# Walking the columns of two feed-forward parts in runs taken from both halves of the tile

## The chip, the cores and the metric

The kernel runs on one core of one Trainium2 chip. The metric is the device time of one execution in microseconds, and lower is better. Engines are named as the profile names them: PE is TensorE (PEld its weight loads), DVE is VectorE, ACT is ScalarE, POOL is GpSimd, SP issues the DMAs.

## The reference

Two layers of a diffusion transformer in float32 on two streams of 256 tokens, the latent `x` and the context `ctx`, each 1024 wide. Each layer is a feed-forward part, a token mixer (a gated recurrence, an mLSTM and a windowed attention, merged by gates) and a second feed-forward part. Every part has a norm in front, which shift and scale by the conditioning, and a gate behind. Cut to what matters:

```python
def swiglu(h, w1, w3, w2):
    return (jax.nn.silu(h @ w1) * (h @ w3)) @ w2

xl, xc = x, ctx
for l in range(DEPTH):                      # DEPTH = 2
    ctx_out = l < DEPTH - 1
    ml, mc = ...                            # modulations from c and c_ctx
    xl = xl + 0.5 * ml[:, :, 2] * swiglu(ln_mod(xl, ...), ffn_w1[l, 0], ffn_w3[l, 0], ffn_w2[l, 0])
    xc = xc + 0.5 * mc[2] * swiglu(ln_mod(xc, ...), ffn_w1[l, 0], ffn_w3[l, 0], ffn_w2[l, 0])
    yl, yc = token_mixer(ln_mod(xl, ...), ln_mod(xc, ...), ..., ctx_out)
    xl = xl + ml[:, :, 5] * yl
    xl = xl + 0.5 * ml[:, :, 8] * swiglu(ln_mod(xl, ...), ffn_w1[l, 1], ffn_w3[l, 1], ffn_w2[l, 1])
    if ctx_out:
        xc = xc + mc[5] * yc
        xc = xc + 0.5 * mc[8] * swiglu(ln_mod(xc, ...), ffn_w1[l, 1], ffn_w3[l, 1], ffn_w2[l, 1])
return xl
```

The inner width of a feed-forward part is 2816, which is 22 chunks of 128.

## The kernel before

Features lie on the 128 partitions and tokens along the columns. A tile of activations is 512 columns wide: columns 0 to 255 are the latent stream (`LAT`), 256 to 511 the context stream (`CTX`), and `BOTH` is all of them. A PSUM bank holds one such tile in float32.

Products keep float32 accuracy with operands of type float32r: each operand is split into a high and a low part, and one chunk of 128 of the contraction is three matmuls, high by high, high by low and low by high (`mm3`, L255 to L263). The weights are the stationary operand, a 128x128 block for each matmul. The activations are the moving operand, `hh` and `hl` (the normed input) or `gh` and `gl` (the inner activations), and the three matmuls add into `ps`. In the profile a matmul of the first kind stands under L261, of the second under L262, of the third under L263.

A feed-forward part (`ffn`, L565) goes through the inner width in three thirds of 8, 7 and 7 chunks (`THIRDS`, L24). In each third, the up products of a chunk make two banks, `p1` and `p3` (L600, L601; the profile writes `p`), over 8 chunks of the contraction; ACT and DVE turn them into `gh` and `gl`. The down products (`dn`, L623 and L638) then contract over the third's 8 or 7 chunks into 8 chunks of the residual. With both streams, up and down products take all 512 columns in one matmul, with two exceptions: the first three chunks of the first third are taken stream by stream (256 columns) where the norm ends stream by stream (`proj_first`, L517, with `BY_STREAM`), and so are the last five chunks of the residual in the last third (`passes_of`, L536).

Of the four feed-forward parts, `(l, j)` = (0, 0), (0, 1) and (1, 0) have both streams; (1, 1) has the latent stream alone, with 256 columns. Parts (0, 1) and (1, 0) follow each other directly, and the mixer of layer 1 follows part (1, 0). In that mixer, `unit` (L1151) makes most products over 256 columns, but nine over 512: three of the keys `k`, four of the values `v`, one each of the attention's keys and values (L1172 to L1179), each of 8 chunks and so 24 matmuls.

PE's order is the program's own (`manual_schedule`, L92). The small products of the norms and of the mixer's chains stand between the large ones at places that a step count sets (`tick`, L158), from fixed durations for a product and not from measured ones. Weights come by DMA on SP's queue into three buffers and are split by ACT (L246) and DVE (L247), some products ahead of their use. DVE also works off the conditioning (L387) beside the first three feed-forward parts.

Of the kernel before, what the change touches and what calls it, by code (L numbers as in the profile page):

```python
# [17 lines left out]
T = 512  # L18
# [15 lines left out]
PREP = 3  # L34
LATER = 300
# [4 lines left out]
# steps of the side chains per microsecond of large products, by layer  # L40
# [8 lines left out]
# columns of the constant array  # L49
# [10 lines left out]
# columns of the per-layer vectors  # L60
V_G = 0            # 3 x 8 x 2
V_ADAB = 48        # 72 x 2
V_CW = 192         # 4 chunks x 4 taps
V_CB = 208
V_BA = 212         # d x c
# [6 lines left out]
V_SINK = 243       # 8  # L72
# [4 lines left out]
# projection chunks of w_in in the order in which they are used  # L77
# [6 lines left out]
def body(ctx, tc, ins, out):  # L84
# [29 lines left out]
    def give(n):  # L114
        """n more slots for weights (or fewer, n < 0)"""
        for _ in range(n):
            free[0].append(free[1].pop(0))
        for _ in range(-n):
            free[1].append(free[0].pop())

# [1 line left out]
    banks = [list(range(PE_MAIN)), list(range(PE_MAIN, 8))]  # L122
# [13 lines left out]
    def pgive(n):  # L136
        """n more banks for the large products (or fewer, n < 0)"""
        a, b = (1, 0) if n > 0 else (0, 1)
        for _ in range(abs(n)):
            banks[b].append(banks[a].pop(0))  # L140

    # ---- small work that runs beside the large products. The tensor engine works in the order of this program:
    # what needs it waits for the end of a large product, so that its operands are there when its turn comes ----
# [4 lines left out]
    def defer(n, f):  # L148
        """call f after n large products"""
        later.append([n, f])  # L150

    def start(gen, rate):
        """a chain of steps; rate: steps per microsecond of large products"""
        ch = [gen, rate, 0.0]
        chains.append(ch)
        return ch
# [83 lines left out]
    def split_w(r, n):  # L240
        """[128, n] weights, chunks of 128 rows side by side -> float32r parts in tiles of 4 chunks"""
        w = []
        for a in range(0, n, 512):
            e = min(n - a, 512)
            hi, lo = salloc("whi", F32R, 0), salloc("wlo", F32R, 0)
            S.copy(hi[:, :e], r[:, a:a + e])  # L246
            V.tensor_tensor(lo[:, :e], r[:, a:a + e], hi[:, :e].bitcast(F32), op=ALU.subtract)  # L247
            w.append((hi, lo))
        return w
# [4 lines left out]

    def mm3(ps, w, kk, xh, xl, cols, ks=None, koff=0):  # L255
        """ps[:, cols] (+)= w.T x in float32 accuracy: high x high + high x low + low x high"""
        for k in (range(kk) if ks is None else ks):
            hi, lo = w[(k + koff) // 4]
            ws = slice((k + koff) % 4 * P, (k + koff) % 4 * P + P)
            o = ps[:, cols]  # L260
            PE.matmul(o, hi[:, ws], xh[k][:, cols], start=(k == 0), stop=False)  # L261
            PE.matmul(o, hi[:, ws], xl[k][:, cols], start=False, stop=False)  # L262
            PE.matmul(o, lo[:, ws], xh[k][:, cols], start=False, stop=(k == kk - 1))  # L263

    def mm3_beside(ps, w, kk, xh, xl, cols):
        """the same, with a place for small work in the middle; the caller ticks the second half"""
        h = kk // 2
        mm3(ps, w, kk, xh, xl, cols, range(h))
        tick(pe_us(cols, h))
        mm3(ps, w, kk, xh, xl, cols, range(h, kk))  # L270

    def split_act(src, cols=BOTH, name="y"):
        """float32 data in two float32r slots"""
        hi = salloc(name + "h", F32R)
        lo = salloc(name + "l", F32R)
        split_into(hi, lo, src, cols)
        return hi, lo
# [6 lines left out]
    def ada_load(h):  # L284
        """a quarter of the weights of the first two modulations, by chunk of the contraction"""
        src = ins["ada0"]
        if h % 2:
            ts = [salloc("ada0") for _ in range(KD)]
            for k in range(KD):
                nc.sync.dma_start(ts[k][:, :T], src[h, :, k * T:(k + 1) * T])  # L290
            return [(t, 0) for t in ts], lambda: sfree(*ts)
        ts = [ada_tile(src[h, :, i * D:(i + 1) * D]) for i in range(2)]
        r = raw_tile(src[h, :, 2 * D:4 * D], 2 * D)
        return [(ts[k // 2], k % 2 * T) if k < 4 else (r, (k - 4) * T) for k in range(KD)], lambda: None

    def ada_first(w, ps, ks):
        """their products on the idle tensor engine, four column groups at once"""
        for k in ks:
            t, o = w[0][k]
            for j in range(4):  # L300
                PE.matmul(ps[32 * j:32 * j + 32, 0:P], cT[:, k, :], t[:, o + j * P:o + (j + 1) * P],
                          start=(k == 0), stop=(k == KD - 1))
# [19 lines left out]
    def ada_second():  # L322
        """the next modulation on the tensor engine, in steps"""
# [29 lines left out]
    def cond_load():  # L353
        """silu of both conditioning vectors, on every partition"""
# [14 lines left out]
    def ada_steps():  # L369
        """the modulations: features on partitions, sums along the rows of the turned weights"""  # L370
# [8 lines left out]
        for i, (l, m) in enumerate(ADA_MODS):  # L379
            # nothing reads the last of the second layer's for the second stream  # L380
# [31 lines left out]
    def rsqrt(v, shape):  # L412
        """v ** -0.5 of a small tile: a first guess from the exponent bits, then Newton steps"""
# [41 lines left out]
    def norm_rstd(s, use, lag=2):  # L455
        """use(rows of 1 / rms on all partitions), some large products later"""
# [42 lines left out]
    # the first chunks of a projection from h, in the order in which h comes: the columns, the chunks of the  # L499
    # contraction, and how many chunks of features take turns  # L500
# [35 lines left out]
    def passes_of(streams, load, use, ahead=None, begin=None):  # L536
        """the products that end a part: the last chunks stream by stream, so that the next norm of one runs beside
        the other. load(pair of chunks), use(stream or None, chunk, weights)"""
# [26 lines left out]
    def ffn(l, j, streams, order, after, first, ahead, prep=None):  # L565
        """after(s, k): called when chunk k of the residual of stream s is complete"""
# [6 lines left out]
        for ti, (a, b) in enumerate(THIRDS):  # L573
            kk = b - a
            gh, gl = [], []
# [57 lines left out]
            def down_first(ws):  # L633
                # the newest chunk of the contraction comes last
# [32 lines left out]
    def log1p_series(o, e, tmp_alloc):  # L667
        """log(1 + e) for 0 <= e <= 1: 2 atanh(e / (2 + e))"""
# [33 lines left out]
    def rg_scan(l, xps, hs):  # L702
        """convolution, gates and hidden states of both directions, summed, chunk by chunk"""
# [19 lines left out]
        for c in range(4):  # L723
# [3 lines left out]
            for d in range(2):  # L727
# [12 lines left out]
                # log a = -2 y; q = tanh y, e = exp(-2 y) = 2 / (1 + q) - 1:  # L740
                # a = 1 - q (1 + e), sqrt(1 - a a) = sqrt(q) (1 + e)
# [37 lines left out]
    def ml_rows(l, f, li, res):  # L779
        """gate rows; per token: columns G (for keys) and exp(-m) (for queries), and -M as rows in two parts"""  # L780
# [4 lines left out]
        # log sigmoid of the forget gates, tokens on partitions  # L785
# [55 lines left out]
    def mlstm(l, q, k, v1, to, f, li, y, lat_only):  # L841
        """q, k feature-major; v1 token-major with a column of ones; to: the output gates"""
# [5 lines left out]
        for h in range(4):  # L848
# [8 lines left out]
            for s in (2, 3, 0, 1):  # L857
# [4 lines left out]
                for d in range(2):  # L862
                    # ranges of queries that see the key chunk s; the mask covers its own chunk
# [30 lines left out]
            for t in tcs:  # L894
                ps = palloc("av")
                for d in range(2):
                    # key chunks that the query chunk t sees
# [49 lines left out]
    def attention(l, k2, queries, vts, rq, y, lat_only):  # L947
# [3 lines left out]
        def scores(c, hf, g, ti):  # L951
            """softmax of one chunk of queries over its keys"""
# [27 lines left out]
        def turn(p, pt, nk, ti):  # L980
            """keys to partitions: key chunk s -> columns (s % 2, query chunk) of tile s // 2"""
# [247 lines left out]
    def attend(l, raws, sqs, vts, y, lat_only, held):  # L1229
        """Per head, the rotated queries in two float32r parts, one above the other; per key head, the normalised  # L1230
        and rotated keys, each part twice: two products over 128 rows make all of the float32 scores. The scales of
        the queries stay apart, as columns."""
# [90 lines left out]
    # ================= program =================  # L1323
# [49 lines left out]
    def prep(h):  # L1373
        """the next quarter of the first modulations and of the normed input"""
# [19 lines left out]
    def normer(l, n):  # L1394
        """squares of the new residual; at its end the norm n of layer l"""
# [37 lines left out]
def _chunk_cols(w):  # L1433
    """[K, N] -> [N / 128, 128 (k in chunk), K / 128 * 128]"""
    K, N = w.shape
    return np.ascontiguousarray(w.reshape(K // P, P, N // P, P).transpose(2, 1, 0, 3)).reshape(N // P, P, K)


def _constants():
    c = np.zeros((P, NCONST), np.float32)  # L1440
    c[:, C_ID:C_ID + P] = np.eye(P)
    # rotation: out[i] = sum_j R[j, i] x[j]
# [119 lines left out]
```

## Time and profile before

| | us |
|---|---|
| runs, median (lowest, highest) | 2230.1 (2229.87, 2230.32) |
| span of the profiled execution | 2228.2 |
| PE busy in the span | 2186.7 (98%) |
| DVE busy | 1495.2 (67%) |
| ACT busy | 1021.4 (46%) |
| mean granted TensorE clock | 0.997 |

The span goes from the first to the last instruction of the profiled execution; the median of the runs is 1.9 us above it. Times along the span are in us from its start. A matmul's busy time in the profile is longer than its share of the engine, since matmuls are pipelined: the next one starts before the one before has ended. What a matmul costs is therefore read from the distance between starts, or from a count in a stretch.

### The profile page before, as it was taken

To read this page: it belongs to the slowest core of one execution; us is meant where nothing else is said; L and a number is where in the kernel's file an instruction comes from. 1 tells how busy PE (TensorE), PEld (TensorE's weight loads), DVE (VectorE), ACT (ScalarE), POOL (GpSimd) and SP (SyncE) were. 2 spreads that over 40 slices of the span, in tenths; PEclk is the share of its full clock that TensorE was granted. 3 is DMA by queue.
4 is the path that set the end of the run, shared out by engine and by line. 5 is a ranking of instruction groups with operands and counts; after the bars stand their busy time and mean duration, and the time that the engine had idled before them with its cause. 6 is when DMAs were issued, how large, how long until landed. Compare 5 with 4: busy or idle time off the path is not lost.

```text
span 2228.2 us, 32885 instructions
## 1 busy us (share of the span) xinstructions
PE 2186.7 (98%) x12357; PEld 1856.5 (83%) x12357; DVE 1495.2 (67%) x3605; ACT 1021.4 (46%) x2021; POOL 4.7 (0%) x40
## 2 busy tenths in 40 slices
PE   6999999999999999999999999999999999998999
PEld 5778888977877778998888898888889778998999
DVE  5899834679766645689973368754346987776664
ACT  4322223468575534542222353232335887655553
POOL 0000000000000000000000000000000000000000
PEclk9999999999999999999999999999999999999999
DMA  9665522311111322445552226642222222454552
GB/s 357 227 236 209 188 92 102 109 62 64 65 57 67 114 86 95 152 160 211 210 175 103 77 89 238 247 165 95 88 93 87 88 83 97 141 181 178 209 189 86
DMA packets 74944, 310.30 MB, mean 139 GB/s; under 512 B 7072, under 2 KB 10656, under 8 KB 60704
## 3 DMA queue, kind: packets, MB, share of 16 engines
q1 hardware_dynamic: 74784, 308.19, 39.0%
q8 instruction: 97, 1.59, 0.3%
q14 instruction: 63, 0.52, 0.1%
HBM read 303.97 MB, written 4.19 MB: 138 GB/s over the span
## 4 chain that ended last, share of the span: by engine, by line
PE 91%; DVE 4%; ACT 3%; DMA 1%; issue 1%; SPq 0%; ACTq 0%; DVEq 0%
PE p L261 11%; PE p L262 11%; PE p L263 11%; PE dn L261 6%; PE dn L262 6%; PE dn L263 6%; PE pg L262 3%; PE pg L261 3%; PE pg L263 3%; PE pj L261 3%; PE pj L262 3%; PE pj L263 3%; PE up L261 2%; PE up L262 2%; PE up L263 2%; PE ao L998 1%
## 5 line engine op out<-in xcount | busy, mean ns | idle before, releaser
L246 ACT CAST whi<-raw 128x512 fp32r<-128x512 f32 (+1 forms) x844 | 506.7, 612 | 830.9 <-PE p L262 385.4
L247 DVE TENSOR_TENSOR wlo<-raw,whi 128x512 fp32r<-128x512 f32 (+1 forms) x844 | 564.2, 678 | 362.0 <-ACT whi L246 352.5
L261 PE MATMUL p<-hh,whi 128*128 128x512 f32 (+1 forms) x1216 | 445.4, 366 | 0.5 <-ACT silu L579 0.5
L262 PE MATMUL p<-hl,whi 128*128 128x512 f32 (+1 forms) x1216 | 445.6, 366 | 0.0
L263 PE MATMUL p<-hh,wlo 128*128 128x512 f32 (+1 forms) x1216 | 444.0, 365 | 0.0
L387 DVE SCALAR_TENSOR_TENSOR junk<-ada,cb 128x512 f32<-128x512 f32 x416 | 290.0, 697 | 34.8 <-DMA ada<-ada 27.7
L261 PE MATMUL dn<-gh,whi 128*128 128x512 f32 (+1 forms) x809 | 275.6, 341 | 0.0
L263 PE MATMUL dn<-gh,wlo 128*128 128x512 f32 (+1 forms) x809 | 275.1, 340 | 0.0
L262 PE MATMUL dn<-gl,whi 128*128 128x512 f32 (+1 forms) x809 | 274.9, 340 | 0.0
L261 PEld LDWEIGHTS p<-hh,whi 128*128 128x128 f32 x1216 | 228.4, 188 | 43.1 <-issue 1.2
L263 PEld LDWEIGHTS p<-hh,wlo 128*128 128x128 f32 x1216 | 228.5, 188 | 40.4
L262 PEld LDWEIGHTS p<-hl,whi 128*128 128x128 f32 x1216 | 228.5, 188 | 39.6
L262 PEld LDWEIGHTS dn<-gl,whi 128*128 128x128 f32 x809 | 152.2, 188 | 18.8
L261 PEld LDWEIGHTS dn<-gh,whi 128*128 128x128 f32 x809 | 152.2, 188 | 18.7
L263 PEld LDWEIGHTS dn<-gh,wlo 128*128 128x128 f32 x809 | 152.1, 188 | 18.7
L261 PE MATMUL pj<-hh,whi 128*128 128x512 f32 (+1 forms) x400 | 153.8, 384 | 1.2 <-DVE li L776 1.2
L262 PE MATMUL pj<-hl,whi 128*128 128x512 f32 (+1 forms) x400 | 143.9, 360 | 0.0
L263 PE MATMUL pj<-hh,wlo 128*128 128x512 f32 (+1 forms) x400 | 143.5, 359 | 0.0
L262 PE MATMUL pg<-hl,whi 128*128 128x512 f32 (+1 forms) x384 | 129.9, 338 | 0.0
L261 PE MATMUL pg<-hh,whi 128*128 128x512 f32 (+1 forms) x384 | 129.8, 338 | 0.0
L263 PE MATMUL pg<-hh,wlo 128*128 128x512 f32 (+1 forms) x384 | 129.3, 337 | 0.0
L496 DVE SCALAR_TENSOR_TENSOR x<-dn,Ga,x 128x256 f32<-128x256 f32 x168 | 74.8, 479 | 54.1 <-PE dn L263 53.4
(281 smaller groups left out, 3444.5 us busy)
## 6 DMA issues: line engine op xcount, KB each, us to landing
raw<-w SPq DMA_DIRECT2D x104, 1024.0 KB, 4.8
ada<-ada SPq DMA_DIRECT2D x124, 512.0 KB, 3.8
raw<-win SPq DMA_DIRECT2D x30, 1024.0 KB, 4.8
raw<-w SPq DMA_DIRECT2D x32, 896.0 KB, 4.6
raw<-wbr SPq DMA_DIRECT2D x24, 1024.0 KB, 4.8
raw<-wbo SPq DMA_DIRECT2D x24, 512.0 KB, 3.3
raw<-wout SPq DMA_DIRECT2D x8, 1024.0 KB, 4.7
raw<-ada SPq DMA_DIRECT2D x6, 1024.0 KB, 6.4
```

The source lines that it names most:

```text
L246: S.copy(hi[:, :e], r[:, a:a + e])
L247: V.tensor_tensor(lo[:, :e], r[:, a:a + e], hi[:, :e].bitcast(F32), op=ALU.subtract)
L261: PE.matmul(o, hi[:, ws], xh[k][:, cols], start=(k == 0), stop=False)
L262: PE.matmul(o, hi[:, ws], xl[k][:, cols], start=False, stop=False)
L263: PE.matmul(o, lo[:, ws], xh[k][:, cols], start=False, stop=(k == kk - 1))
L387: V.scalar_tensor_tensor(junk[0], r[:, e * T:(e + 1) * T], 1.0, cb[2 * s + e][:, :T], op0=ALU.mult, op1=ALU.mult, accum_out=am[:, b, s, e: ...
L496: V.scalar_tensor_tensor(x[k][:, c], ps[:, c], Gate[l, n][:, k, s:s + 1], x[k][:, c], op0=ALU.mult, op1=ALU.add)
L998: PE.matmul(po[c][rows, cc], vts[0][:, sv * P + 64 * hf:sv * P + 64 * hf + 64], pt[s // 2][:, (s % 2) * 256:(s % 2) * 256 + 256], start=(s ...
```

## The change

In `ffn`, each third sets `walk[0]` from the table `WALKS`; parts that aren't in the table set 0. In `mm3`, a product over 512 columns whose `walk[0]` is not 0 no longer goes through columns 0 to 511 in order. Its moving operand and its output are seen as `(h b r) -> b h r`: `r` columns of the first half, the same `r` columns of the second half, the next `r` of the first half, and so on. Operand and output go through the columns in the same order, so each column's result lands where it did. Products over 256 columns are as before. Comments and docstrings were dropped as well, which moves line numbers: L261 to L263 become L270 to L272.

```diff
+WALKS = {(0, 1): (128, 32, 4), (1, 0): (64, 16, 8)}
...
+    walk = [0]
+
     def mm3(ps, w, kk, xh, xl, cols, ks=None, koff=0):
         for k in (range(kk) if ks is None else ks):
             hi, lo = w[(k + koff) // 4]
             ws = slice((k + koff) % 4 * P, (k + koff) % 4 * P + P)
-            o = ps[:, cols]
-            PE.matmul(o, hi[:, ws], xh[k][:, cols], start=(k == 0), stop=False)
-            PE.matmul(o, hi[:, ws], xl[k][:, cols], start=False, stop=False)
-            PE.matmul(o, lo[:, ws], xh[k][:, cols], start=False, stop=(k == kk - 1))
+            run = walk[0] if cols.stop - cols.start == T else 0
+
+            def v(t):
+                a = t[:, cols]
+                return a.rearrange("p (h b r) -> p b h r", h=2, r=run) if run else a
+            o = v(ps)
+            PE.matmul(o, hi[:, ws], v(xh[k]), start=(k == 0), stop=False)
+            PE.matmul(o, hi[:, ws], v(xl[k]), start=False, stop=False)
+            PE.matmul(o, lo[:, ws], v(xh[k]), start=False, stop=(k == kk - 1))
...
         for ti, (a, b) in enumerate(THIRDS):
             kk = b - a
+            walk[0] = WALKS.get((l, j), (0, 0, 0))[ti]
```

On PE, at the start of the last third of part (0, 1), the three matmuls of the first two chunks of `p1` stand like this before; `hh` and `hl` are the normed input, `whi` and `wlo` the weights:

```order
L261 MATMUL p_2016_10629<-hh_87,whi_10613 128x512
L262 MATMUL p_2016_10629<-hl_95,whi_10613 128x512
L263 MATMUL p_2016_10629<-hh_87,wlo_10614 128x512
L261 MATMUL p_2016_10629<-hh_88,whi_10613 128x512
L262 MATMUL p_2016_10629<-hl_96,whi_10613 128x512
L263 MATMUL p_2016_10629<-hh_88,wlo_10614 128x512
```

The same place of PE after the change, where 64 blocks of two runs of 4 columns make up the 512:

```order
L270 MATMUL p_2016_10629<-hh_87,whi_10613 128x64x2x4
L271 MATMUL p_2016_10629<-hl_95,whi_10613 128x64x2x4
L272 MATMUL p_2016_10629<-hh_87,wlo_10614 128x64x2x4
L270 MATMUL p_2016_10629<-hh_88,whi_10613 128x64x2x4
L271 MATMUL p_2016_10629<-hl_96,whi_10613 128x64x2x4
L272 MATMUL p_2016_10629<-hh_88,wlo_10614 128x64x2x4
```

Nothing moved: the same matmuls stand in the same order, and only the way through the columns differs. On DVE, ACT, POOL and SP every instruction stands where it stood, with the shape that it had.

The last value of the table, 8 from the last third of part (1, 0), stays in `walk[0]` until part (1, 1) begins. On PE, in the mixer of layer 1, the first of the nine products over 512 columns (`pj`, here a key chunk) reads after the change, behind a product over 256 columns and a transposition of the gates (`ft`):

```order
L272 MATMUL pj_15223<-hh_94,wlo_15220 128x256
L794 MATMUL ft_15257<-con,f_15183 128x128 x4
L270 MATMUL pj_15276<-hh_87,whi_15268 128x32x2x8
L271 MATMUL pj_15276<-hl_95,whi_15268 128x32x2x8
L272 MATMUL pj_15276<-hh_87,wlo_15269 128x32x2x8
L270 MATMUL pj_15276<-hh_88,whi_15268 128x32x2x8
```

So 216 matmuls outside the two feed-forward parts are walked in runs of 8 as well, and again nothing is moved.

The matmuls concerned, counted from the loops (three matmuls for each chunk of each product):

| part, third | stretch in the profile before, us | run | matmuls |
|---|---|---|---|
| (0, 1), first | 973.4 to 1073.7 | 128 | 240 up + 192 down = 432 |
| (0, 1), second | 1073.7 to 1190.5 | 32 | 336 + 168 = 504 |
| (0, 1), third | 1190.5 to 1283.0 | 4 | 336 + 63 = 399 |
| (1, 0), first | 1345.4 to 1445.6 | 64 | 432 |
| (1, 0), second | 1445.6 to 1562.5 | 16 | 504 |
| (1, 0), third | 1562.5 to 1655.0 | 8 | 399 |
| mixer of layer 1 | 1721 to 1843 | 8 | 9 x 24 = 216 |

## Rows read from the trace of the kernel before

**Rows 1.** The page, parts 1 and 2: the span, PE, its granted clock.
```profile
span 2228.2 us, 32885 instructions
...
PE 2186.7 (98%) x12357; PEld 1856.5 (83%) x12357; DVE 1495.2 (67%) x3605; ACT 1021.4 (46%) x2021; POOL 4.7 (0%) x40
...
PEclk9999999999999999999999999999999999999999
```

**Rows 2.** The page, part 4: the chain that ended last, shares of the span.
```profile
PE 91%; DVE 4%; ACT 3%; DMA 1%; issue 1%; SPq 0%; ACTq 0%; DVEq 0%
```

**Rows 3.** Windows, PE alone: six thirds, a stretch of 256-column products, the mixer.
```profile
core 0: us, PE busy (x), PEclk, DMA share, GB/s
973.40:1073.70 100.30, 100.30 (x435) 1.00 0.59 216
1073.70:1190.50 116.80, 116.80 (x506) 1.00 0.51 176
1190.50:1283.00 92.50, 92.50 (x401) 1.00 0.25 87
1345.40:1445.60 100.20, 100.20 (x434) 1.00 0.68 245
1445.60:1562.50 116.90, 116.90 (x505) 1.00 0.37 130
1562.50:1655.00 92.50, 92.50 (x400) 1.00 0.27 90
2100.00:2200.00 100.00, 100.00 (x847) 1.00 0.48 172
1721.00:1843.00 122.00, 118.14 (x662) 1.00 0.25 84
```

**Rows 4.** Timeline of PE where the third with run 4 begins.
```profile
1190.49 0.40 PE L261 MATMUL p<-hh,whi 128*128 128x512 f32 x1
1190.73 0.39 PE L262 MATMUL p<-hl,whi 128*128 128x512 f32 x1
1190.96 0.39 PE L263 MATMUL p<-hh,wlo 128*128 128x512 f32 x1
1191.19 0.40 PE L261 MATMUL p<-hh,whi 128*128 128x512 f32 x1
```

**Rows 5.** The longest waits between 973 and 1283 us: who waited for whom, total, times.
```profile
ACT whi L246 <- PE p L262: 111.1, 62, 2.3
ACT whi L246 <- PE dn L262: 65.8, 33, 3.7
```

**Rows 6.** Float32 products of the recurrence's gates: timeline of two; line L732, min/median/max ns.
```profile
1778.02 1.88 PE L732 MATMUL rg<-u,rgw 128*128 128x512 f32 x4
...
L732 PE MATMUL rg<-u,rgw x64: 590/592/697, 455.9 to 1805.2; 128*128 128x512 f32 x64
```

**Rows 7.** ACT exponentials over 32 columns: L835 in runs of 4, L791 in one.
```profile
L835 ACT ACTIVATE em<-gt x2: 230/230/231, 486.7 to 1750.1; 128x32 f32<-128x32 f32 x2
...
L791 ACT ACTIVATE fe<-fe x2: 229/230/230, 455.8 to 1723.6; 128x32 f32<-128x32 f32 x2
```

**Rows 8.** DVE over 32 columns: L788 reads PSUM in runs of 4, L670, L672 without gaps.
```profile
L788 DVE COPY fc<-ft x2: 191/192/194, 454.1 to 1721.8; 128x32 f32<-128x32 f32 x2
...
L670 DVE TENSOR_SCALAR fz<-fe 128x32 f32<-128x32 f32 x1 | 0.2, 183 | 1.3 <-ACT fe L791 1.3
...
L672 DVE TENSOR_TENSOR fz<-fz,fe 128x32 f32<-128x32 f32 x1 | 0.2, 193 | 0.0
```

## The prediction

> **What bounds the kernel now.** I read the page's busy shares first, then the chain that ended last, then windows cut at the thirds of the two feed-forward parts, then the timeline at one border. PE is busy for 98% of the span, at a granted clock that reads 9 in every slice [rows 1], and it makes up 91% of the chain [rows 2]. In the six stretches that the change touches, PE is busy without a break and the granted clock is 1.00, the upper of its two levels [rows 3]; the others wait for it, ACT for instance 111.1 us in all for up products to release weight buffers [rows 5]. So every nanosecond that a product gains or loses there goes into the time one for one, and nothing hides it.
>
> What a product costs is the distance between starts, 0.23 to 0.24 us in the timeline [rows 4], and not its busy 0.39 us. From the windows: the six stretches last 100.3 + 116.8 + 92.5 + 100.2 + 116.9 + 92.5 = 619.2 us and hold 432 + 504 + 399 products, twice, so 2670; 619.2 / 2670 = 231.9 ns. The counts of the windows are a few higher because products at the edges count twice. A product over 256 columns costs 100 / 847 = 118.1 ns [rows 3]. The difference, 113.8 ns for 256 columns, is 0.4445 ns a column, which leaves 231.9 - 512 x 0.4445 = 4.3 ns for each product beside its columns.
>
> **What the change removes, adds and moves.** It removes nothing and moves nothing. Per walked product it adds borders between runs: a run of r columns gives 512 / r runs, of which the first is not a border. There are 2886 walked products: the 2670, and 216 of the mixer of layer 1 that inherit run 8. Runs in all: 432 x 4 (run 128) + 432 x 8 (64) + 504 x 16 (32) + 504 x 32 (16) + 615 x 64 (8) + 399 x 128 (4) = 1728 + 3456 + 8064 + 16128 + 39360 + 51072 = 119,808. Less the 2886 first ones, 116,922 borders. More than two fifths of them lie in the one third with run 4, and 0.1 ns a border is 11.7 us of the time.
>
> The sum has one unknown, the price of a border (or of a walked product as such), since no matmul of the trace goes through its columns with gaps. Bounds:
>
> - Upper, by the border: it should not cost more than what a new product costs beside its columns, with its weights and its start, 4.3 ns. 116,922 x 4.3 ns = 503 us, so 2733 us.
> - Upper, by the product: PE has a slower way of streaming in this trace. The float32 products of the recurrence's gates run in two passes each, and four passes in a row take 1.88 us of which the last lasts 0.592 [rows 6]: (1.88 - 0.592) / 3 = 0.429 us a pass, against 0.2319. If walked products fell to that pace, each would cost 197 ns more, 2886 x 197 = 570 us, so 2800 us.
> - Lower, below nothing: half of that pass is 0.2147 us, so a product over 512 columns at exactly twice the slow pace would be 17.2 ns shorter than it is. If the new walk took away whatever costs these 17.2 ns, the gain would be 2886 x 17.2 = 50 us, so 2180 us.
> - What stands nearest in pattern, on other engines: ACT's exponential over 32 columns in eight runs of 4, read from SBUF with gaps of 28 and more, takes 230 ns, and the same function over 32 columns without gaps 230 [rows 7]; maximum against minimum they differ by 2 ns, under 0.3 ns for each of seven borders. DVE reads eight runs of 4 out of PSUM in 192 ns; 32 columns without gaps take it 183 ns with one operand and 193 with two, both from SBUF [rows 8].
>
> I take nothing for a border, by these last rows: they are the only ones with the same pattern, runs of four float32 with gaps, on either memory, and they show a price of 0 to 1.3 ns (ACT: none, DVE: at most 9 ns over seven borders), of which I take ACT's, where both rows are one operation. They are other engines at a slower pace than 0.44 ns a column, so they speak for the address walk and not for PE's pace; that keeps both ends in the range. Every run here starts at a multiple of its own length and is at least 4 columns long, so no run leaves a pair of columns split.
>
> The notes speak on both sides. The Trainium skill, Advanced Engine Details and Errata, section PSUM Cachelines, says that "any non-contiguous AP significantly slows down matmuls"; by that sentence all 2886 products would be slow, and no run here shows it. Its next sentence asks only that each two consecutive elements be contiguous, and the SBUF section beside it wants two hits on a 16-byte line; runs of 4 float32 satisfy both, and by these the sum stays at nothing. ACT's and DVE's equal times [rows 7, 8] agree with the second reading, and are no test of the first, which speaks of matmuls.
>
> Consumers of the banks (silu, the residual's update) read the same columns after the last matmul, as before, and transfers and splits are paced by PE, so nothing else changes. The sum: 2228.2 us of span + 1.9 us around it (the median of the runs less the span) + 0 = 2230 us.
>
> **The rivals.**
> - *A border costs a column.* The walk loses one column's time, 0.4445 ns, at each border: 116,922 x 0.4445 = 52 us, 2282 us. For it: a stream of one column per step has no slack for a restart. Against it: ACT's rows, with under 0.3 ns. With half or twice the price it is 2256 to 2334 us. The point from which it decides is 0.38 ns a border, where it passes 2%. The third with run 4 would carry 399 x 127 x 0.4445 = 22.5 us of it.
> - *Short runs fall to the slow pace.* Runs of 4 and 8, 399 + 399 + 216 = 1014 products, go at 0.429 us: + 200 us, 2430 us. For it: the shortest runs give a fetch the least to work with. Against it: nothing in the rows of ACT or DVE shows such a step.
> - *Every walked product falls to the slow pace.* + 570 us, 2800 us, the same for run 128 as for run 4. For it: 0.429 us is a pace that PE does have. Against it: in the trace it goes with two-pass float32 operands, not with a walk. This is what the first sentence quoted from the Trainium skill above would do here.
> - *The walk helps.* Something costs the float32r products 17.2 ns above twice the slow pace, perhaps reads of weights and activations that meet; another order might part them: - 50 us, 2180 us. Against it: the other readers don't change, and the distances in the timeline are even [rows 4].
>
> **How the numbers follow.** No price: 0.63. A column per border (with half or twice that): 0.15. Short runs slow: 0.08. All slow: 0.09. Helps: 0.05. The forecast is that of the first, 2230 us; its own range is 2226 to 2247, the upper end from ACT's resolution at 0.14 ns a border (1 ns over seven). The whole range goes from 2215, a part of the helping case, to 2335, the border at twice a column: 0.63 + 0.15 + 0.02, some 0.80. A difference of 2%, 45 us, is about what a measurement of this kernel can tell from no change. Slower than that: 0.08 + 0.09 + two thirds of the border case, 0.10, together 0.27. Faster: 0.03, the larger part of the helping case. Within 2%: the remaining 0.70.
>
> **What would show it.** Right: each of the six stretches as long as before to 0.3 us, 231.9 ns a product in all of them, and the nine products of the mixer unchanged. A price per border shows as stretches that grow with 512 / r, the third with run 4 twice as much as that with run 8, and the first thirds by almost nothing; a pace that falls shows as products at 0.43 us, in the short runs alone or in all. The forecast is wrong if any stretch is more than 1 us longer or shorter.

## The result, and the profile after

The changed kernel takes 2249.85 us (median of 2248.35 and 2251.35) against 2230.1 us: a ratio of 1.0088, 95% interval 1.0069 to 1.0107. That is 20 us slower: inside the range that was given and under 2%, but clear of the scatter, where no change had been forecast.

The page of the changed kernel, its head, answers to [rows 1]:

```profile
span 2249.6 us, 32885 instructions
...
PE 2207.7 (98%) x12357; PEld 1861.4 (83%) x12357; DVE 1495.6 (66%) x3605; ACT 1022.2 (45%) x2021; POOL 4.7 (0%) x40
...
PEclk9999999999999999999999999999999999999999
```

PE is busy 21.0 us longer (2207.7 against 2186.7) in a span that is 21.4 us longer. DVE and ACT do what they did, and the granted clock has not fallen. The windows of the changed kernel, cut at the same places of the program as [rows 3], say where; the last row is the mixer from its first product behind the recurrence's to its first gate product:

```profile
core 0: us, PE busy (x), PEclk, DMA share, GB/s
973.70:1074.00 100.30, 100.30 (x434) 1.00 0.61 216
1074.00:1193.20 119.20, 119.20 (x506) 1.00 0.48 172
1193.20:1293.40 100.20, 100.20 (x400) 1.00 0.23 82
1355.90:1456.10 100.20, 100.20 (x435) 1.00 0.68 243
1456.10:1577.20 121.10, 121.10 (x505) 1.00 0.35 125
1577.20:1674.20 97.00, 97.00 (x400) 1.00 0.25 86
1737.50:1893.00 155.50, 150.12 (x878) 0.99 0.24 79
```

Against [rows 3], run 128 and run 64 add 0.0 us, run 32 adds 2.4, run 16 4.2, run 8 4.5 and run 4 7.7: 18.8 us. The mixer took 154.1 us before, from 1718.3 to 1872.4, and adds some 1.3; PE's busy time in it grows by 2.3 us (147.8 to 150.1), about what 216 products at 11 ns more make, so PE waits 1 us less there. The last 1.3 us of the span lie where no product is walked and are not assigned; the two runs of the changed kernel differ by 3, and the profile is of the slower one. By product (the stretch over the count from the loops): 100.2 / 399 = 251.1 ns with run 4, 97.0 / 399 = 243.1 with run 8, 121.1 / 504 = 240.3 with run 16, 119.2 / 504 = 236.5 with run 32, 231.9 to 232.2 with 64 and 128, where the straight walk had 231.9.

The timeline at the place of [rows 4]:

```profile
1193.18 0.41 PE L270 MATMUL p<-hh,whi 128*128 128x512 f32 x1
1193.42 0.41 PE L271 MATMUL p<-hl,whi 128*128 128x512 f32 x1
1193.67 0.42 PE L272 MATMUL p<-hh,wlo 128*128 128x512 f32 x1
1193.93 0.42 PE L270 MATMUL p<-hh,whi 128*128 128x512 f32 x1
```

Starts lie 0.24 to 0.26 us apart instead of 0.23 to 0.24: every product is a little longer, none is held up.

### The profile page after: what moved, and what is told of

It reads as the page before. It is cut to its first block, busy times and chain, and to the rows that moved or that the text cites. A ratio compares the mean times of both kernels' runs of the same rounds, so it can differ in the third digit from the quotient of the medians.

```text
span 2249.6 us, 32885 instructions
## 1 busy us (share of the span) xinstructions
PE 2207.7 (98%) x12357; PEld 1861.4 (83%) x12357; DVE 1495.6 (66%) x3605; ACT 1022.2 (45%) x2021; POOL 4.7 (0%) x40
## 4 chain that ended last, share of the span: by engine, by line
PE 91%; DVE 4%; ACT 3%; DMA 1%; issue 1%; SPq 0%; ACTq 0%; DVEq 0%
PE p L270 11%; PE p L271 11%; PE p L272 11%; PE dn L270 6%; PE dn L271 6%; PE dn L272 6%; PE pg L271 3%; PE pg L270 3%; PE pg L272 3%; PE pj L270 3%; PE pj L271 3%; PE pj L272 3%; PE up L270 2%; PE up L271 2%; PE up L272 2%; PE ao L1008 1%
## 5 line engine op out<-in xcount | busy, mean ns | idle before, releaser
L270 PE MATMUL p<-hh,whi 128*128 128x512 f32 (+1 forms) x1216 | 451.1, 371 | 0.5 <-ACT silu L589 0.5
L271 PE MATMUL p<-hl,whi 128*128 128x512 f32 (+1 forms) x1216 | 451.3, 371 | 0.0
L272 PE MATMUL p<-hh,wlo 128*128 128x512 f32 (+1 forms) x1216 | 450.0, 370 | 0.0
L270 PE MATMUL dn<-gh,whi 128*128 128x512 f32 (+1 forms) x809 | 277.5, 343 | 0.0
L272 PE MATMUL dn<-gh,wlo 128*128 128x512 f32 (+1 forms) x809 | 276.9, 342 | 0.0
L270 PEld LDWEIGHTS p<-hh,whi 128*128 128x128 f32 x1216 | 229.6, 189 | 46.8 <-issue 1.2
L272 PEld LDWEIGHTS p<-hh,wlo 128*128 128x128 f32 x1216 | 229.6, 189 | 44.2
L270 PEld LDWEIGHTS dn<-gh,whi 128*128 128x128 f32 x809 | 152.6, 189 | 19.8
L272 PEld LDWEIGHTS dn<-gh,wlo 128*128 128x128 f32 x809 | 152.6, 189 | 19.7
L270 PE MATMUL pj<-hh,whi 128*128 128x512 f32 (+1 forms) x400 | 155.0, 387 | 1.2 <-DVE li L786 1.2
L272 PE MATMUL pj<-hh,wlo 128*128 128x512 f32 (+1 forms) x400 | 144.5, 361 | 0.0
L270 PE MATMUL pg<-hh,whi 128*128 128x512 f32 (+1 forms) x384 | 130.0, 339 | 0.0
L272 PE MATMUL pg<-hh,wlo 128*128 128x512 f32 (+1 forms) x384 | 129.5, 337 | 0.0
```

The source lines that it names most:

```text
L270: PE.matmul(o, hi[:, ws], v(xh[k]), start=(k == 0), stop=False)
L271: PE.matmul(o, hi[:, ws], v(xl[k]), start=False, stop=False)
L272: PE.matmul(o, lo[:, ws], v(xh[k]), start=False, stop=(k == kk - 1))
```

## The experiments

All start from the changed kernel. In the diffs the table holds, per third, the number of parts from which runs are taken, the run, and whether the walk is used where the moving operand is read and where PSUM is written. From these kernels rows are shown for the up products of the six thirds alone (240, 336, 336 in each part), cut from their first start to the first start of the down products. The product's time is the stretch over that count. Each of these kernels ran once, apart from the two for which a time is given, which ran four times.

**Which side pays.**

```diff
-WALKS = {(0, 1): (128, 32, 4), (1, 0): (64, 16, 8)}
+WALKS = {(0, 1): ((2, 4, 1, 0), (2, 4, 0, 1), (2, 32, 1, 0)),
+         (1, 0): ((2, 32, 0, 1), (2, 16, 1, 0), (2, 16, 0, 1))}
...
-            o = v(ps)
+            o = v(ps, 3)
```

> The walk is done on one side at a time: in the six thirds, in order, run 4 when read, run 4 when written, run 32 when read, run 32 when written, run 16 when read, run 16 when written (the other side goes straight). Columns of these products therefore land in another order, so the output is not the reference's. The mixer's products are not walked. In the changed kernel a product cost 251.2 ns with run 4, 240.4 with run 16 and 236.4 with run 32, against 231.9. Theory R, the price is paid where the moving operand is read from SBUF: 251, 232, 236, 232, 240, 232 ns. Theory W, it is paid where PSUM is written: 232, 251, 232, 236, 232, 240. Theory B, both sides pay and the larger one shows: each of the six lies above 232, and neither side alone reaches the sum.

Windows of that kernel:

```profile
973.70:1034.10 60.40, 60.40 (x243) 1.00 0.59 211
1082.40:1160.30 77.90, 77.90 (x338) 1.00 0.61 209
1199.20:1278.70 79.50, 79.50 (x338) 1.00 0.25 88
1356.00:1411.60 55.60, 55.60 (x242) 1.00 0.68 242
1456.20:1536.80 80.60, 80.60 (x337) 1.00 0.40 139
1577.30:1655.20 77.90, 77.90 (x337) 1.00 0.26 90
```

252, 232, 237, 232, 240, 232 ns: theory R, within a nanosecond. The whole price is paid where the moving operand is read; writing PSUM in runs is free.

**Whether the place matters.** The same walk, the runs at other places: `((2, 4, 1, 1), (2, 16, 1, 1), (2, 64, 1, 1))` and `((2, 8, 1, 1), (2, 32, 1, 1), (2, 128, 1, 1))`.

> The walk on both sides as in the changed kernel, with the runs at other places: 4, 16, 64 in part (0, 1) and 8, 32, 128 in part (1, 0); the mixer's products are not walked. Theory run length (the price goes by the run alone): 251, 240, 232, 243, 236, 232 ns a product. Theory company (the price comes from what DVE, ACT and the DMAs do beside the products, heaviest in the first two thirds of each part): the first third at run 4 costs clearly more than 251, run 8 in the first third of the other part more than 243, and run 32 at its new place another price than 236.

```profile
974.90:1035.20 60.30, 60.30 (x243) 1.00 0.60 211
...
1359.70:1418.10 58.40, 58.40 (x243) 1.00 0.69 237
1464.80:1544.30 79.50, 79.50 (x337) 1.00 0.39 135
```

Run 4 in the busy first third costs 251 ns, run 8 at its new place 243, run 32 237. With run 4 the DMAs are busy for 0.60 of that stretch, and for 0.23 of the third where run 4 stood before. What DVE, ACT and the DMAs do meanwhile has no part in it that shows.

**How far the next run lies.** Run 4 on both sides, taken from 4, 8, 16, 32, 64 and 128 parts: `((4, 4, 1, 1), (8, 4, 1, 1), (16, 4, 1, 1))` and `((32, 4, 1, 1), (64, 4, 1, 1), (128, 4, 1, 1))`.

> Run 4 everywhere, taken in turn not from halves but from 4, 8, 16, 32 and 64 parts of the tile, so that runs taken one after the other are 128, 64, 32, 16 and 8 columns apart instead of 256; the last third has 128 parts of one run each, which is the straight order. Order of reading and writing is the same, so columns land where they did. Theory border (each border costs the same however far the next run is): 251 ns in the first five thirds and 232 in the last. Theory distance (what costs is leaving a stretch of memory that is 64 columns long, since runs of 64 and more were free): the price falls with the distance, to about 240 or less where the next run is 8 or 16 columns on. Theory row (alternation between the same two stretches 1 KB apart is what costs): 232 wherever there are more than two parts.

```profile
973.90:1038.10 64.20, 64.20 (x242) 1.00 0.58 201
1089.60:1182.90 93.30, 93.30 (x337) 1.00 0.52 176
1229.60:1311.70 82.10, 82.10 (x338) 1.00 0.24 84
1389.50:1443.50 54.00, 54.00 (x242) 1.00 0.70 248
1487.10:1565.20 78.10, 78.10 (x338) 1.00 0.44 148
```

268, 278, 244, 225 and 232 ns with the same run and the same number of borders (and 232 in the last third, the straight order): a border has no fixed price of its own. None of the three theories holds. Distance matters, but 64 columns is dearest, and at 16 columns the walk is cheaper than the straight one.

**Shorter runs.** `((2, 2, 1, 1), (2, 2, 1, 0), (2, 2, 0, 1))` and `((2, 1, 1, 0), (2, 8, 1, 0), (2, 8, 0, 1))`.

> Shorter runs: in part (0, 1) run 2 on both sides, run 2 when read, run 2 when written; in part (1, 0) run 1 when read, run 8 when read, run 8 when written. Where one side alone is walked, columns land in another order and the output is not the reference's. The mixer's products are not walked. Theory border (a fixed price a border, 0.15 ns as at run 4): run 2 costs 255 borders x 0.15 = 38 ns more, 270 ns, and run 1 when read 511 x 0.15 = 77, 309 ns. Theory line (the price comes from fetching 16 bytes at a time, of which a run of 2 uses half and a run of 1 a quarter): run 2 goes at half the pace, 430 ns or more, and run 1 at a quarter. Run 8 alone: 243 on the side that pays, 232 on the other.

```profile
973.60:1053.30 79.70, 79.70 (x242) 1.00 0.48 165
1116.70:1228.10 111.40, 111.40 (x337) 1.00 0.43 147
1283.70:1361.60 77.90, 77.90 (x337) 1.00 0.25 88
1438.60:1490.40 51.80, 51.80 (x242) 1.00 0.71 256
...
1654.40:1732.30 77.90, 77.90 (x337) 1.00 0.26 90
```

Run 2 costs 332 ns when read, 232 when written; run 8 costs 243 when read and 232 when written (the last line). And run 1, which both theories called the dearest, costs 51.8 / 240 = 216 ns, 16 less than the straight walk. Both theories fall.

**Run 1 and run 2 at other distances.** Read alone. Run 1 from 4, 8, 16, then 64, 128, 256 parts; and run 2 from 4, 8, 16, then 32, 64, 128 parts.

> Run 1 when read, output straight, so columns land in another order and the output is not the reference's. Runs one after the other are 128, 64, 32 columns apart in the thirds of part (0, 1), 8, 4, 2 in part (1, 0); part (1, 1), whose products have 256 columns, reads run 1 at 128 and at 64 apart and run 4 at 128. Run 1 at 256 apart was 215.8 ns in the run before, less than the straight walk's 231.9. Theory single (a read column by column has no shared fetch to lose, whatever the distance): 216 ns in all six thirds, and 108, 108 and about 130 ns in part (1, 1), against 118.1. Theory distance (the price goes by how far the next column lies, as it did at run 4, where 64 columns apart were dearest): dearer than 232 at 128 and 64 apart, cheap at 8 and less. Theory resonance (moving reads meet the weight reads at a rhythm): no order by distance; some of the six at 216, others above 232.

> Run 2 when read, output straight (columns land in another order), with runs one after the other 128, 64, 32 columns apart in part (0, 1) and 16, 8, 4 in part (1, 0); part (1, 1) with 256 columns reads run 16 at 128 apart, run 4 at 32 and run 2 at 128. Run 2 at 256 apart was 331 ns. Theory distance: the same order as run 4 had by distance (256: 251, 128: 268, 64: 278, 32: 244, 16: 225, 8: 232), only with twice the surplus over 216: about 320, 340, 270, 235, 250. Theory alternation (a pair that is not followed by its neighbour costs a fetch): about 330 in all six.

Windows of the first two thirds with run 1, then of the first with run 2:

```profile
974.60:1041.20 66.60, 66.60 (x243) 1.00 0.55 192
1094.60:1258.50 163.90, 163.90 (x338) 1.00 0.30 105
```

```profile
973.60:1080.40 106.80, 106.80 (x243) 1.00 0.37 131
```

Run 1 costs 278 and 488 ns, and in the other thirds 431 to 461; run 2 445, and in the others 436 to 488. All at a granted clock of 1.00. Only two parts are cheap for run 1, over 256 columns too (112 ns from two parts, 142 from four), so "single", "distance" and "resonance" fall. For run 2, "distance" falls as well; "alternation" is right that all six are dear, but not in size, with every value above 430 where it wanted about 330.

**Whether the weights' reads take part.** The moving operand straight in part (0, 1), weights read with steps 0, 2, 4; in part (1, 0) run 4, 4, 16 with steps 0, 4, 0.

```diff
-            PE.matmul(o, hi[:, ws], v(xh[k]), start=(k == 0), stop=False)
+            hw, lw = wv(hi), wv(lo)
+            PE.matmul(o, hw, v(xh[k]), start=(k == 0), stop=False)
```

> The weights' read is changed instead: in part (0, 1) the moving operand goes straight while the weights of the products over eight chunks are read at one address (step 0), every second and every fourth column of their tile; in part (1, 0) the moving operand has run 4, run 4, run 16 and the weights step 0, 4, 0; part (1, 1) with 256 columns goes straight with weights at step 0, 2, 4. The products use other weights, so the output is not the reference's. Theory resonance (the 17 ns above 215 of the straight walk, and the price of run 4 and 16, come from moving reads that meet the weight reads of the next product): step 0 brings the straight walk to 216 and 107 ns, and run 4 and run 16 below 251 and 240, and steps 2 and 4 give other values than 232. Theory moving (the price is the moving operand's own): 232, 232, 232, then 251, 251, 240, and 118 for all of part (1, 1).

Windows of the first third of part (0, 1) (step 0), its last (step 4), the first of part (1, 0) (run 4, step 0) and the first of part (1, 1) (256 columns, step 0):

```profile
973.60:1029.10 55.50, 55.50 (x243) 1.00 0.64 222
...
1190.70:1270.10 79.40, 79.40 (x337) 1.00 0.26 88
1347.20:1406.90 59.70, 59.70 (x243) 1.00 0.67 236
...
2075.60:2102.90 27.30, 27.30 (x241) 1.00 0.69 246
```

231, 236 and 249 ns against 232, 232 and 251. Over 512 columns the weights shift the values by a few ns and carry neither the price of the runs nor the 16 ns: the moving operand's own read does. Over 256 columns that does not hold: with step 0 a product takes 27.3 / 240 = 113.8 ns, where the same third took 119.2 before (28.6 / 240), so there the weights' read has a part that no run separates from the moving operand's. (Step 4 doubles a product over 256 columns to 235 ns; each weight load lasts 332 ns there instead of 188.)

**A theory for the moving operand's read.** Of the columns of a walk, those at even places and those at odd places are fetched as two streams; a fetch brings four neighbouring columns; and a product goes the faster the more of the four its stream uses in a row. Run 1 from two halves gives each stream four (216 ns), the straight walk and aligned runs of 4 or more give two (225 to 278), run 2, and run 1 from more parts, one (278 to 488). It gives the order of these kinds, and not the differences within one. The next two runs were made to fell it.

**Neighbouring stretches in turn.** Run 1 from two stretches that are 128, 64, 32, then 16, 8, 4 columns apart (the line taken out is that of the kernels with such a table).

```diff
-                    return a.rearrange("p (h b r) -> p b h r", h=wk[0], r=wk[1])
+                    return a.rearrange("p (g h b) -> p g b h", g=wk[0], h=2)
```

> Run 1 when read, taken in turn from two neighbouring stretches: the columns go a0 b0 a1 b1 ... with a and b 128, 64, 32 columns apart in part (0, 1), 16, 8, 4 apart in part (1, 0), and 64, 16, 4 apart in the 256-column products of part (1, 1). Output straight, so columns land in another order and the output is not the reference's. Theory two streams (columns at even and at odd places of the walk are fetched apart, a fetch brings four neighbours, and what counts is how many of the four its own stream uses in a row: four cost nothing, 216 ns; two, as the straight walk and run 4 have them, 16 to 60; one, run 2 and run 1 over more than two parts, 60 to 270): near 216 ns at every distance, since each stream uses all four, apart from some ns that go by the distance; 108 to 112 in part (1, 1). Theory halves (alternation 1 KB apart is special in itself): 216 at no distance of these, and values like the 278 to 488 of run 1 with more than two parts.

```profile
973.50:1025.30 51.80, 51.80 (x242) 1.00 0.64 222
...
1537.00:1609.50 72.50, 72.50 (x338) 1.00 0.28 96
...
2068.90:2106.40 37.50, 37.50 (x338) 1.00 0.53 185
```

72.5 / 336 = 215.8 ns at every distance, and 37.5 / 336 = 111.6 over 256 columns (the last line). The last third of part (1, 0) takes four columns here and four right beside them, in the order a0 b0 a1 b1: the same memory as the straight walk, in another order, and 16 ns less.

**Runs that start off a fetch.** The normed input's tiles are 4 columns wider, and up products read from column 2. (Part (0, 1): straight from 0, run 4 from 2, run 1 from 2; part (1, 0): straight from 0, run 4 from 0, run 8 from 2.)

```diff
-                a = t[:, cols]
+                a = t[:, cols.start + off:cols.stop + off]
```

> The tiles of the normed input are 4 columns wider, and the up products read them from a later column on, so that columns are off by some and the output is not the reference's. Up products: part (0, 1) straight from column 0, run 4 from column 2, run 1 (halves) from column 2; part (1, 0) straight from 0, run 4 from 0, run 8 from 2; part (1, 1), 256 columns, straight from 2, run 4 (128 apart) from 2, run 4 from 1. Down products start at column 0. Theory two streams with fetches of four columns: run 4 from column 2 lies over two fetches of which each stream uses one column, so it costs as much as run 2, about 331 ns against 251; run 8 from column 2 lies between, 260 to 300 against 243; run 1 from column 2 stays at 216, since each stream still uses all four; in part (1, 1) 118, then about 167 (the price of run 2 there) for run 4 from 2 and more than 128 from 1. Theory run length (only the run counts, not where it starts): 232, 251, 216, 232, 251, 243, and 118, 128, 128.

```profile
1073.80:1186.00 112.20, 112.20 (x337) 1.00 0.44 150
1228.10:1300.80 72.70, 72.70 (x338) 1.00 0.28 96
...
1477.10:1561.90 84.80, 84.80 (x338) 1.00 0.39 134
1604.00:1720.90 116.90, 116.90 (x337) 1.00 0.19 64
```

Run 4 from column 2 costs 112.2 / 336 = 334 ns, where 331 was expected, against 252 from column 0. Run 1 stays at 216. Run 8 from 2 costs 348, more than the 260 to 300 expected and far from run length's 243. That is a miss of the theory in size and in order: its streams use more of a fetch here than with run 4 from column 2, and yet the product is dearer. Over 256 columns run 4 costs 169 from column 2 and 168 from 1, against 128 aligned; 167 was expected from 2.

**The version that uses it.** All products read in turn from both halves, and the split parts are stored for that: even tokens in the first half, odd ones in the second.

```diff
+    def apart(t, cols):
+        return t[:, 0:T].rearrange("p (h b) -> p h b", h=2)[:, :, cols.start // 2:cols.stop // 2]
+    def paired(t, cols):
+        return t[:, cols].rearrange("p (b h) -> p h b", h=2)
+    def in_turn(t, cols):
+        return t[:, 0:T].rearrange("p (h b) -> p b h", h=2)[:, cols.start // 2:cols.stop // 2]
...
+            o = ps[:, cols].rearrange("p (b h) -> p b h", h=2)
+            PE.matmul(o, hi[:, ws], in_turn(xh[k], cols), start=(k == 0), stop=False)
...
-        S.copy(hi[:, cols], src[:, cols])
-        V.tensor_tensor(lo[:, cols], src[:, cols], hi[:, cols].bitcast(F32), op=ALU.subtract)
+        S.copy(apart(hi, at), paired(src, cols))
+        V.tensor_tensor(apart(lo, at), paired(src, cols), apart(hi, at).bitcast(F32), op=ALU.subtract)
```

> All products of the kernel, over 512 and over 256 columns, read their moving operand in turn from both halves, one column at a time; the high and low parts are stored so that this gives the order of the tokens (even tokens in the first half, odd ones in the second), and the output goes straight, so PSUM and everything behind it are as before. ACT and DVE read every second column when they split activations. If the 216 ns of run 1 hold for all 512-column products and 107 to 112 for those over 256: 5965 x 16 ns = 95 us and 5078 x 6 to 11 ns = 30 to 56 us less, so 2079 to 2105 us, a ratio of 0.932 to 0.944. If ACT's and DVE's reads at every second column cost more than they have to spare before the first products of a part, some us less. If the gain of run 1 was an effect of the other order of the results, no gain: 2230.

2142.1 us against 2232.3 for the kernel before on the same chip, a ratio of 0.960 (0.9584 to 0.9616): it beats both kernels, by less than was expected. The second thirds' down products of the parts (0, 0) and (0, 1), and PE's longest wait:

```profile
237.80:290.20 52.40, 42.55 (x169) 0.87 0.48 171
1109.40:1155.90 46.50, 38.88 (x169) 0.89 0.45 159
```

```profile
PE dn L271 <- ACT gh L291: 17.4, 4, 7.6
```

At 216 ns, 168 products would take 36.3 us; here they take 52.4 and 46.5. PE waits up to 7.6 us for the last inner chunk, and the mean granted clock of the two stretches is 0.87 and 0.89; in the first, behind a wait of 4.9 us, starts lie 0.43 us apart for a while instead of 0.22. In all, PE is busy for 116 us less than in the kernel before (2070.7 against 2186.7), in a span that is 88.1 us shorter, so 28 us went into PE's waits; 125 to 151 us had been expected. DVE's conditioning steps, in the same queue as the split, are the first suspect: the products got faster than DVE works them off.

**Whether DVE's queue is it.**

```diff
-FEEDS = {(0, 0): 42, (0, 1): 40, (1, 0): 40}
+FEEDS = {(0, 0): (42, 42, 42), (0, 1): (40, 20, 20), (1, 0): (55, 55, 55)}
```

> The version that reads in turn everywhere, with the conditioning's steps on DVE spread further: part (0, 1) feeds at the rates 40, 20, 20 in its thirds instead of 40, and part (1, 0) at 55 instead of 40. Before it, 2142.1 us, with the down products of the second third of part (0, 1) at 278 ns and those of its first third at 227 because PE waited for DVE's and ACT's split of the last inner chunk and then ran at a lower granted clock. If DVE's queue of conditioning steps is what delayed that split: 168 x (278 - 216) + 192 x (227 - 216) = 10 + 2 us less, about 2130 us, unless part (1, 0) takes the delay over. If the split itself is what is late: no change.

```profile
1106.70:1142.90 36.20, 36.20 (x169) 1.00 0.30 114
1455.10:1504.00 48.90, 39.85 (x168) 0.90 0.46 167
```

Part (1, 0) in the version before it:

```profile
1468.00:1504.10 36.10, 36.10 (x170) 1.00 0.31 116
```

2145.5 us, ratio 0.962 (0.9604 to 0.9636): nothing gained in all. The stall left part (0, 1), 36.2 us, and came back in part (1, 0), where the same stretch took 36.1 us in the version before and now takes 48.9. The delay goes where the steps go.

**Where the price of runs 4 to 32 comes from.** Halves 260, 264, 272 apart with run 4, then 272 apart with runs 8, 16, 32.

```diff
+                if off and wk[on]:
+                    a = t[:, 0:2 * off].rearrange("p (h c) -> p h c", h=2)[:, :, 0:TL]
+                    return a.rearrange("p h (b r) -> p b h r", r=wk[1])
                 a = t[:, cols]
```

> The tiles of the normed input are 32 columns wider, and the up products of the six thirds read halves that start 260, 264 and 272 columns apart with run 4 (part (0, 1)) and 272 apart with runs 8, 16, 32 (part (1, 0)), so that the second half is not the context stream's columns and the output is not the reference's; the output of these products goes straight. Down products keep halves 256 apart, and 251 to 236 ns. So far the price of run 4 went with the share of jumps that are a multiple of 64 columns (64 apart 278 ns, 128 apart 268, 256 apart 251, 8 and 16 apart 232 and 225). Theory places (memory is divided into places that repeat every 64 columns, and a fetch from a place used shortly before waits; the straight walk comes back after 16 fetches of four columns, run 32 after 8, run 16 after 4, run 8 after 2, run 4 at once): at 260 apart the next fetch of the first half meets the place just used, about 251; at 264 and 272 it does not, 235 or less; run 8 at 272 comes back after 6, about 237; run 16 and run 32 at 272 meet within the same few fetches, 236 to 243. Theory border (each border has a price of its own, wherever the next run lies): 251, 251, 251, then 243, 240, 236.

```profile
972.50:1032.10 59.60, 59.60 (x243) 1.00 0.61 213
1080.40:1162.20 81.80, 81.80 (x337) 1.00 0.58 200
1204.30:1285.40 81.10, 81.10 (x338) 1.00 0.25 86
...
1589.80:1670.70 80.90, 80.90 (x337) 1.00 0.26 86
```

248, 243 and 241 ns with run 4, where "places" wanted 251, 235 and 235, and run 32 at 272 costs 241, more than its 236 at 256 apart; runs 8 and 16 stay at 242 and 241. Half of run 4's surplus goes with the distance, half stays. Neither theory holds as a whole: how the surplus of aligned runs splits between them is left open.

## Why the prediction was wrong

**What bounds the kernel: right.** PE's 21.0 us are the span's 21.4. In the six thirds nothing hid them; in the mixer, where PE also waits, 1 of 2.3 us was hidden.

**The step that failed** is "I take nothing for a border, by these last rows". ACT's and DVE's reads in runs of 4 [rows 7, 8] said nothing of PE's read of its moving operand, and that is where the price was paid. The measured surplus is 19 ns a product at run 4 (0.15 ns for each of 127 borders), 11 at run 8, 8.4 at run 16, 4.6 at run 32 and none at 64 and 128. That is 18.8 us over the six thirds, or 0.18 ns for each of their 116,922 - 216 x 63 = 103,314 borders, where 0 was taken and 0.4445 was the rival's price. The 2249.85 us lie between the forecast's own range, which ended at 2247, and the border rival's, which began at 2256.

**The form was wrong too.** "A border costs a column" was the nearest rival, with the right sign and the right order of thirds, and is not what happens: the price is not proportional to the borders (0.15 ns for each at run 4, 0.18 at run 8, 0.27 at run 16, 0.31 at run 32), and at one run it goes from -7 to +46 ns with the distance of the next. The check that I had named, the third with run 4 growing twice as much as that with run 8, gives 7.7 against 4.5 us.

**The bounds held for this walk.** The upper one by the product is no bound for walks at large: run 1 from 8 parts costs 256 ns more than the straight walk, where the slow pace made 197. Of the 17.2 ns of "the walk helps", 16 are there to be had, at run 1, but not by this walk. I had called that case unlikely, among other things because the distances between starts were even; even distances say only that every product pays alike. And the 0.4445 ns a column held part of that price already: with run 1 the same difference is (215.8 - 111.6) / 256 = 0.407.

**The other rivals fell.** No product fell to 0.43 us at a run of 4 or more that starts on a multiple of four columns. Shorter runs from more than two parts did and passed it (431 to 488, but 278 for run 1 from 4 parts); shifted runs of 4 and 8 reached 334 and 348.

**The two sentences of the Trainium skill** (Advanced Engine Details and Errata, Memory Cachelines) come out differently. That any access pattern in PSUM which isn't contiguous slows matmuls: the runs differ. Outputs in runs of 2, 4, 8, 16 and 32 cost 232 ns, as the straight one does. That SBUF wants two hits on a 16-byte line: counted in the order of the walk, the runs differ, since run 2 and run 4 from column 2 have two hits in a row and cost 332 and 334 ns, and run 1 from halves never has two in a row and costs 216. Counted for each stream of the model above, the runs agree in kind, 334 ns with one hit and 252 with two for the same run 4, from column 2 and from column 0; but two are not the whole of it, since four give 216. The prediction took the second rule for a licence; runs of 4 and more that start on a multiple of four escaped only the large loss (225 to 278 ns, against 332 to 488 with run 2 and shifted runs).

**Shown and not shown.** Shown: the price is on the moving operand's read, does not depend on the other engines, and over 512 columns falls to 216 ns, the least of all, in each walk tried in which every second column runs on through neighbours. That there are two streams and fetches of four columns is a model; it foretold 334 and 216 ns before they were measured, and missed run 8 from column 2 in size and in order. Why aligned runs cost 225 to 278 ns by their distance and length is open, and so is how the weights' read shares in the time over 256 columns.

## What to carry to other kernels

What a walk costs an engine must be measured on that engine: rows of another engine with the same pattern are no bound. A matmul's even cadence at a full granted clock can still hold a price (here 232 ns, where 216 could be had): try another order of reading the moving operand. Storing it so that two stretches are read in turn, one column each, took 4% off this kernel. When the bound gets faster, look at once for the helper that was just fast enough: here DVE's side work, whose delay moved with it from part to part.

## What was not expected of the hardware

- One column each from two stretches is faster than the straight read: 215.8 against 231.9 ns over 512 columns, 111.6 against 118.1 over 256 [rows 3], whether the stretches are 4 or 256 columns apart.
- Run 2 costs 332 ns and run 1 from 8 parts 488, at a full granted clock: a stretch at half pace is not always a lowered clock.
- Weights read at one address take 5.4 ns off a product over 256 columns (119.2 to 113.8) and nothing off one over 512 (231 against 232).
- Writing PSUM in runs down to 2 columns costs nothing (232 ns).
- Reading every second column does cost ACT and DVE something when they split activations. Lines of the version that reads in turn, ACT's and DVE's:

```profile
L291 ACT CAST gh<-silu 128x512 fp32r<-128x512 f32 x66 | 56.3, 852 | 216.1 <-DVE silu L590 216.1
...
L292 DVE TENSOR_TENSOR gl<-silu,gh 128x512 fp32r<-128x512 f32 x66 | 54.1, 820 | 11.1 <-ACT gh L291 11.0
```

They took 622 and 690 ns when reading straight. ACT's casts also waited longer for DVE, 216.1 us in all against 88.2 before.
